# Keeping the residual of a four-layer decoder trunk transposed, and writing the mixer outputs transposed

## The chip, the cores and the metric

The kernel runs on one core of one Trainium2 chip. The metric is the device time of one launch in microseconds (us), lower is better. Three runs of the kernel before took 1474.31, 1475.74 and 1479.85 us; their median, 1475.74 us, is the time to compare with. The engines are named as the profile names them: PE (matrix products; PEld is its weight load), DVE (vector), ACT (scalar), POOL, and SP, which only starts transfers here.

## The reference

256 tokens of 1024 numbers pass through two layers of a mixer and an expert stage; every part adds its result to a residual `h`.

```python
h = x
for layer in range(2):
    xn = rmsnorm(h, norm_mix[layer])
    if layer == 0:
        h = h + attn_retention_mixer(xn, even_w_in, even_w_out)   # q, k, v, gate: 1024 -> 3584; out 1024 -> 1024
    else:
        h = h + short_conv_mixer(xn, odd_w_in, odd_conv, odd_w_out)  # 1024 -> 3072, gates, 3-tap conv, 1024 -> 1024
    h = h + peer(rmsnorm(h, norm_ffn[layer]), w_q, sub_keys, u, v)
return rmsnorm(h, final_norm)
```

`rmsnorm(x, g)` is `x / sqrt(mean(x*x) + eps) * g`. `peer` makes 8 query heads per token, takes the top 16 of 256 candidate experts of each head out of 16384 experts, and sums `gate * gelu(t . u[e]) * v[e]` over them.

## The kernel before, in words

**Precision.** Most products of full precision are three products: each factor is split into a high part (a cast on ACT, L176 for weights) and a low part in bf16 (a subtraction on DVE or POOL, L178). For an activation the high part and the remainder lie side by side in `x2` (8 blocks of 128 model dimensions, two parts, 256 tokens), a bf16 copy of the high part in `Xb`, cast by POOL.

**Weights.** `Stream` holds a list of all weight tiles in their order of use and a ring of 8 raw tiles of 512 KB. `st.next()` hands out the next tile and first calls `st.ahead`, which loads and splits tiles up to two beyond it; `st.parts()` splits one more; `st.next(ahead=False)` and `st.loads()` only take or load. The order of the instructions on every engine is the order of the program text: each engine takes its own in turn, and waits on semaphores for the others.

**Four stages, then four more.** (1) The even mixer: 28 weight tiles, attention and retention worked in between, then the output projection. (2) The expert stage `peer` of layer 0. (3) The odd mixer: 24 input tiles, convolution, output projection. (4) `peer` of layer 1, and the last norm.

**Output projection of a mixer** (`v_phase`, `v_mm`, L324 to L358). The result has the tokens on the partitions: four accumulators of 128 tokens by 512 dimensions, one PSUM bank each. The activation is the stationary operand, 128 columns of it, and the weight tile moves, 512 columns a product. Each of the eight weight tiles gives 12 products. The last two tiles are worked accumulator by accumulator, so that the four quarters of the result come out one after another.

**The norm behind a mixer** (`Norm`). Each quarter is added to `h` by DVE (L356), squared on ACT with a row sum (L397), and turned by PE, four transposes a call of `turn` (L445), because the next stage needs the model dimensions on the partitions. `parts` then makes `x2` (ACT L454, DVE L455) from the turned blocks. The transposes stand between the products of the last two weight tiles and inside the first pair of query tiles. `u_pair` (L308) multiplies two weight tiles with `x2` block by block and calls `tail(k)` behind each block k. The scale of the norm is applied later, to the scores.

**The expert stage.** For each of 16 query tiles f: a query product (`u_tile`), a copy to `qT` (L1312), and, one f later, the product with the keys (L1160), whose result is scaled on its way out of PSUM (L1163). `pump` deals the routing (top 16 of the scores, then of the pairs, the search for indices, the gates) to DVE in small pieces. For 160 of the 256 tokens the experts are worked densely: all 128 tiles of `u` (`dense_u`, L1417), the gelu, then all 128 tiles of `v` (L1520, L1560, L1562) into eight accumulators `vo`, one PSUM bank for each 128 model dimensions. For the other 96 tokens, rows of `u` and `v` are fetched by address (POOL L1029) and summed on DVE (L1039, L1050); `leave` (L1537) turns these sums into `vo`. `rows` (L522) makes what both paths read: `whole` and `scaled` (L528, L532) the dense activation out of `x2`, `fetched` (L535) the normalised rows out of `h`, `doubled` copies of them.

**The residual at the end of `peer`.** In steps 16 to 23 of the dense `v` phase PE adds the residual to `vo`, by a product of a block of `h` with the identity (L1550, L1551). The last three `v` tiles are worked block by block; `fold` (L1572) brings a block out of PSUM with an ACT copy (L1573) and a DVE sum of 160 columns (L1574) into `XT`, which is transposed. Behind layer 0, `Folded` makes `x2` out of `XT` (L576, L577) and has PE turn `XT` back in four groups of four transposes (`back`, L548), for the squares (L593) and for `h` (L609). Behind layer 1, `Final` squares the blocks, multiplies them with the gain, turns them and scales them.

**The start.** `x` comes with the tokens on the partitions in two transfers, one from SP and one from ACT; the small constants come before it, three weight tiles after it, all from SP. PE turns `x` (16 transposes), and `first` makes `x2` from the turned blocks with three weight splits in between; `late` sums the squares of `h` in steps 0 and 1.

The lines that a sentence does not say, the body of the projection before:

```python
for a in range(4):
    for j in range(2):
        run(v_mm(ws[j], ps[j], accs[a], a // 2, a % 2, False, j == 1))
        if a == 3 and j == 0:
            norm.amid()
    v.tensor_tensor(h[:, a // 2, ...], accs[a], h[:, a // 2, ...], OP.add)
    norm.done(a, accs[a])
```

## Time and profile before

| what | value |
|---|---|
| median of three runs | 1475.74 us (1474.31 to 1479.85) |
| the profiled execution, its own time | 1473.25 us |
| its span, first to last instruction | 1471.5 us |
| PE, PEld busy | 97%, 90% of the span |
| DVE, ACT, POOL busy | 84%, 55%, 53% |
| granted PE clock | 0.996 |
| read from memory | 527.93 MB, 359 GB/s over the span |
| even mixer, first product to last | 9.8 to 128.6 us |
| expert stage of layer 0 | 128.6 to 746.7 us |
| odd mixer | 746.7 to 844.2 us |
| expert stage of layer 1 and last norm | 844.2 to 1471.5 us |

How to read it: times in the rows are microseconds from the start of the span. A row of the timeline gives start, duration, engine, line, operation, output and inputs with their shapes, and the count that is merged into the row; behind it in brackets stands how long the engine had been idle, and what released it. PE's products are pipelined: one lasts some 0.3 to 0.6 us from end to end, but the next one starts much earlier. So the rate of PE is read from the distance between starts, not from the durations. Outside the span lie 1.75 us of the profiled execution (1473.25 less 1471.5).

### The profile page before, as it was taken

What the parts mean: (1) busy time and instruction counts of PE and PEld (TensorE: products, weight loads), DVE (VectorE), ACT (ScalarE), POOL (GpSimd) and SP (SyncE); (2) the same over time, 40 slices, a digit from 0 to 9 for tenths busy, and PEclk for the clock granted to TensorE, in tenths of its full rate; (3) what the DMA queues carried; (4) which work ended last, traced back from release to release, by engine and by line L of the source; (5) the groups of instructions that cost most, each with busy time, mean ns of one, the idle gap of its engine ahead of it and who ended that gap; (6) DMA issues with size and microseconds to landing.
All of it is one profiled execution on the core that took longest, in us unless ns stands there. A gap on an engine that the chain in (4) does not pass through costs nothing.

```text
span 1471.5 us, 29881 instructions
## 1 busy us (share of the span) xinstructions
PE 1426.3 (97%) x11246; PEld 1327.1 (90%) x11260; DVE 1238.5 (84%) x2505; ACT 804.0 (55%) x1872; POOL 779.3 (53%) x508
## 2 busy tenths in 40 slices
PE   9999999999999999999999999999999999999997
PEld 5667999999999999988998699999999999998887
DVE  5637999968898689989976589998788869999997
ACT  5555512248786556665563463212887746665654
POOL 6754545555655247655444374465555626665440
PEclk9999999999999999999999999999999999999999
DMA  8546899999999999999975588999999999999994
GB/s 325 191 156 247 315 370 392 400 414 411 409 406 404 400 393 412 415 416 414 411 264 181 180 303 342 403 382 406 409 412 413 410 411 392 408 415 414 415 415 181
DMA packets 113729, 531.78 MB, mean 361 GB/s; under 512 B 13168, under 2 KB 13424, under 8 KB 83888
## 3 DMA queue, kind: packets, MB, share of 16 engines
q1 hardware_dynamic: 57024, 325.06, 55.8%
q0 software_dynamic: 56416, 204.29, 35.1%
q8 instruction: 88, 1.44, 0.4%
q10 hardware_dynamic: 144, 0.52, 0.1%
q14 instruction: 57, 0.47, 0.1%
HBM read 527.93 MB, written 1.05 MB: 359 GB/s over the span
## 4 chain that ended last, share of the span: by engine, by line
PE 37%; DVE 23%; DMA 23%; issue 9%; POOL 6%; ACT 1%; DVEq 0%; SPq 0%; POOLq 0%; ACTq 0%
PE hid L1417 11%; DMA grow<-pvn,ig 9%; DMA rows<-pvn,ig 9%; PE vo L1560 5%; DMA rows<-pun,ig 4%; POOL rows L1029 4%; DVE rows L1039 4%; PE vo L1562 3%; PE hid L299 2%; PE vo L1520 2%; DVE hg L1149 2%; DVE hg L1155 2%; DVE hg L1151 2%; POOL grow L1029 2%; PE ea L331 2%
## 5 line engine op out<-in xcount | busy, mean ns | idle before, releaser
L1417 PE MATMUL hid<-xf,raw 128*128 128x160 f32 x3328 | 477.2, 301 | 7.8 <-DVE hg L1460 7.8
L1417 PEld LDWEIGHTS hid<-xf,raw 128*128 128x128 f32 x3328 | 457.8, 190 | 10.0 <-DVE hg L1460 9.9
L1428 ACT CAST vhi<-raw 128x1024 fp32r<-128x1024 f32 x222 | 229.9, 1047 | 191.7 <-DMA raw<-pv 96.7
L1029 POOL DMA_INDIRECT rows<-pvn,ig x128 | 217.7, 1700 | 183.9 <-DVE gacc L1050 150.1
L1435 DVE TENSOR_TENSOR vlo<-raw,vhi 128x1024 bf16<-128x1024 f32 x222 | 266.5, 1216 | 22.5 <-ACT vhi L1428 22.1
L1029 POOL DMA_INDIRECT rows<-pun,ig x128 | 163.4, 1277 | 116.1 <-DVE rows L1039 59.1
L1560 PE MATMUL vo<-ko,vhi 128*128 128x320 f32 x1200 | 213.6, 320 | 0.0
L178 POOL TENSOR_TENSOR lo<-raw,hi 128x1024 bf16<-128x1024 f32 x70 | 168.0, 2410 | 85.1 <-ACT hi L176 77.2
L1560 PEld LDWEIGHTS vo<-ko,vhi 128*128 128x128 f32 x1200 | 178.0, 189 | 0.0
L1562 PE MATMUL vo<-hb,vlo 128*128 128x160 bf16 x1776 | 162.0, 234 | 15.8 <-DVE vlo L1435 15.6
L1050 DVE SCALAR_TENSOR_TENSOR gacc<-rows,ghid,gacc 128x1024 f32<-128x1024 f32 x124 | 158.3, 1277 | 17.9 <-DMA rows<-pvn,ig 17.6
L1039 DVE SCALAR_TENSOR_TENSOR rows<-rows,xg 128x1024 f32<-128x1024 f32 x128 | 154.9, 1217 | 21.2 <-DMA rows<-pun,ig 20.9
L1029 POOL DMA_INDIRECT grow<-pvn,ig x64 | 117.7, 1838 | 94.7 <-DVE gacc L1050 77.2
L1457 ACT ACTIVATE hg<-hid 128x160 f32<-128x160 f32 (+14 forms) x240 | 61.9, 265 | 192.3 <-PE hid L1417 192.2
L1562 PEld LDWEIGHTS <-vlo 128*128 128x128 bf16 x1776 | 117.9, 98 | 42.4 <-DVE vlo L1435 22.2
L1029 POOL DMA_INDIRECT grow<-pun,ig x64 | 84.2, 1316 | 79.0 <-DVE grow L1039 51.9
L1367 ACT ACTIVATE ko<-ko,idxT 128x128 f16<-128x128 f16 x320 | 101.6, 391 | 38.3 <-DVE ko L1352 38.2
L176 ACT CAST hi<-raw 128x1024 fp32r<-128x1024 f32 x100 | 102.3, 1046 | 29.0 <-issue 17.4
L299 PE MATMUL hid<-x,hi 128*128 128x256 f32 x800 | 107.4, 287 | 3.9 <-DVE z L982 2.0
L299 PEld LDWEIGHTS hid<-x,hi 128*128 128x128 f32 x800 | 98.6, 190 | 5.0 <-issue 3.1
L1560 PE MATMUL vo<-xf,vhi 128*128 128x320 f32 x576 | 102.7, 321 | 0.0
L1370 ACT ACTIVATE ko<-ko,idxT 128x128 f16<-128x128 f16 x320 | 101.2, 389 | 0.0
(258 smaller groups left out, 2238.4 us busy)
## 6 DMA issues: line engine op xcount, KB each, us to landing
raw<-pv SPq DMA_DIRECT2D x128, 1024.0 KB, 9.4
raw<-pu SPq DMA_DIRECT2D x104, 1024.0 KB, 8.2
raw<-wq SPq DMA_DIRECT2D x32, 512.0 KB, 4.0
raw<-ew_in SPq DMA_DIRECT2D x28, 512.0 KB, 4.6
raw<-ow_in SPq DMA_DIRECT2D x24, 512.0 KB, 4.9
hg<-pe_ SPq DMA_DIRECT2D x22, 512.0 KB, 6.4
raw<-ew_out SPq DMA_DIRECT2D x8, 512.0 KB, 4.0
raw<-ow_out SPq DMA_DIRECT2D x8, 512.0 KB, 3.5
```

The lines of the kernel that those rows point to most:

```text
L176: self.nc.scalar.copy(hi, t)
L178: eng.tensor_tensor(lo, t, hi.bitcast(F32), OP.subtract)
L299: pe.matmul(ps[:, :S], hi[:, k * P:(k + 1) * P], A2[:, k, s_, :], start=k == 0 and s_ == 0, stop=False)
L1029: gp.indirect_dma_start(self.row(s_), None, table, bass.IndirectOffsetOnAxis(IG[:, 0, s_ % STEPS:s_ % STEPS + 1].bitcast(U32), 0))
L1039: v.scalar_tensor_tensor(r, r, 1.0, XG[:, q % 2, :], op0=OP.mult, op1=OP.mult, accum_out=w)
L1050: v.scalar_tensor_tensor(self.acc[q], r, w, self.acc[q], op0=OP.mult, op1=OP.add)
L1367: act.activation(hi[:, j], lo[:, j], AF.Copy, scale=idxT[:, 1, t:t + 1])
L1417: pe.matmul(ps[:, :TD], w[k], xv["xf"][:, k, :], start=k == 0, stop=k == ND - 1)
L1428: act.copy(whi[j], raw)
L1435: v.tensor_tensor(wlo[j], raw, whi[j].bitcast(F32), OP.subtract)
L1560: pe.matmul(vo[b][:, TG:S + TD], hi[:, b * P:(b + 1) * P], hs, **m)
L1562: pe.matmul(vo[b][:, TG:S], lo[:, b * P:(b + 1) * P], hb, **m)
```

## The change

`h` is now transposed from the first load to the last norm: 128 model dimensions on the partitions, eight blocks of 256 tokens. The host gives `x` in that form, and a second copy `xn` with the tokens on the partitions, which only the first norm's sums read.

- **Start.** The two halves of `x` and then the two of `xn` are loaded by ACT, the small table by POOL, three weight tiles and the constants by SP. PE turns nothing; `first` makes `x2` from `h` straight away. 28 idle products instead of 24 keep PE running before. `late` runs in steps 1 and 2.
- **Output projection.** The weight tile is stationary, the activation moves: per weight tile 16 products of the high part (two for each of eight blocks) and then eight of the low part, each with 256 columns. Block b lies in accumulator b % 4, half b // 4. The split of the first two query tiles is asked for one tile earlier (`st.ahead(2)`). The last two weight tiles are worked block by block.
- **Norms behind a part.** `Norm` serves all four: behind each block one or two DVE sums into `h`, ACT's high part, ACT's square (not summed), DVE's low part. Two DVE sums in `tail(2)` add the squares up over the blocks, and four products with a column of ones (`sums`, L540 of the changed kernel) add them up over the partitions, behind `u_pair` and ahead of whatever PE does next. There are no transposes between.
- **Expert stage.** `fetched_rows` turns the 96 fetched tokens back (eight transposes) and scales them. `dense` makes the dense activation in eight DVE operations of 160 columns, in place of one sum and one product of 1280. The products with the identity are gone; `fold` is two DVE operations.
- **Last norm.** The gain is applied by ACT, not DVE.

```diff
-    h = pers.tile([P, 2, D], F32, tag="h", name="h")
+    h = pers.tile([P, ND, S], F32, tag="h", name="h")
...
         accs = [acc_tile(i, nm("acc")) for i in range(4)]
+        def out_of(b):
+            return accs[b % 4][:, b // 4 * S:(b // 4 + 1) * S]
+        def high(b, w, p, first):
+            c = slice(b * P, (b + 1) * P)
+            m = dict(stop=False, skip_group_check=True)
+            pe.matmul(out_of(b), w[0][:, c], p[0], start=first, **m)
+            pe.matmul(out_of(b), w[0][:, c], p[1], start=False, **m)
+        def low(b, w, p, last):
+            pe.matmul(out_of(b), w[1][:, b * P:(b + 1) * P], p[2], start=False, stop=last, skip_group_check=True)
         for i in range(n - 2):
             each(i)
             w = st.next()
+            if i == n - 3:
+                st.ahead(2)
             p = part(i)
-            for a in range(4):
-                run(v_mm(w, p, accs[a], a // 2, a % 2, i == 0, False))
+            for b in range(ND):
+                high(b, w, p, i == 0 and b < 4)
+            for b in range(ND):
+                low(b, w, p, False)
...
-        ws = [st.next(), st.next(ahead=False)]
-        st.ahead(0)
+        ws = [st.next(ahead=False) for _ in range(2)]
+        st.loads()
...
+        norm.begin(lambda b: v.tensor_tensor(h[:, b, :], out_of(b), h[:, b, :], OP.add))
+        for b in range(ND):
+            for w, p in zip(ws, ps):
+                high(b, w, p, False)
+            for j, (w, p) in enumerate(zip(ws, ps)):
+                low(b, w, p, j == 1)
+            norm.block(b, [])
...
+    def fetched_rows(norm):
+        fq = [acc_tile(ch, nm("fq")) for ch in range(2)]
+        for b in range(ND):
+            pe.transpose(fq[b // 4][:TG, b % 4 * P:(b % 4 + 1) * P], h[:, b, :TG], ident)
+        for ch in range(2):
+            c = slice(ch * 512, (ch + 1) * 512)
+            v.scalar_tensor_tensor(XG[:TG, 0, c], fq[ch][:TG, :], norm.scale(0)[:TG], XG[:TG, 1, c],
+                                   op0=OP.mult, op1=OP.mult)
...
+        def block(self, b, pend):
+            self.fold(b)
+            self.high(b)
+            act.activation(self.sq[b // 4][:, b % 4 * S:(b % 4 + 1) * S], h[:, b, :], AF.Square)
+            if b:
+                self.low(b - 1)
+            if b == 5 and self.mixes:
+                st.parts()
+            if b == ND - 1:
+                self.low(b)
+        def tail(self, k):
+            if k == 1:
+                if self.mixes:
+                    st.parts()
+                else:
+                    st.ahead(0)
+            if k == 2:
+                a, b = self.sq
+                v.tensor_tensor(a, a, b, OP.add)
+                v.tensor_tensor(a[:, :2 * S], a[:, :2 * S], a[:, 2 * S:], OP.add)
+            if k == 7 and self.mixes:
+                st.parts()
+                st.parts()
...
+            def dense():
                 XF = new_xf()
                 ps = self.spread()
+                for k in range(ND):
+                    v.scalar_tensor_tensor(XF[:, k, :], h[:, k, TG:], self.gain(k), ps[:, TG:], op0=OP.mult, op1=OP.mult)
...
                 if f == 0:
                     pair = u_pair(xv["x2"], Xb, before.tail)
+                    before.sums()
...
-                m = dict(start=False, stop=False, skip_group_check=True)
-                if 16 <= i < 16 + ND:
-                    b = i - 16
-                    c = slice(b * P, (b + 1) * P)
-                    pe.matmul(vo[b][:, :P], h[:, 0, c], ident, **m)
-                    pe.matmul(vo[b][:, P:S], h[:, 1, c], ident, **m)
...
             def fold(b):
-                act.copy(XT[:, b, :], vo[b][:, :S])
-                v.tensor_tensor(XT[:, b, TG:], vo[b][:, S:S + TD], XT[:, b, TG:], OP.add)
+                v.tensor_tensor(h[:, b, :], vo[b][:, :S], h[:, b, :], OP.add)
+                v.tensor_tensor(h[:, b, TG:], vo[b][:, S:S + TD], h[:, b, TG:], OP.add)
...
-        nc.sync.dma_start(G, small)
-        nc.sync.dma_start(C[:, :P], cst[:, :P])
-        for th in range(2):
-            (nc.scalar if th else nc.sync).dma_start(h[:, th, :], x[th])
-        nc.sync.dma_start(C[:, P:], cst[:, P:])
+        gp.dma_start(G, small)
+        for a in range(2):
+            nc.scalar.dma_start(h[:, a * 4:(a + 1) * 4, :], x[:, a * 4:(a + 1) * 4, :])
...
+        for th in range(2):
+            nc.scalar.dma_start(XG[:, th, :], xn[th])
+        nc.sync.dma_start(C, cst)
-        busy(24)
+        busy(28)
```

Two places show how the order moves. The first is PE at the end of the even mixer, on the last two weight tiles. Before: `acc` is a quarter of the result, `c2e` and `cbe` the activation, `hi` and `lo` the parts of the weights, `xt` the turned residual.

```order
L333 MATMUL acc_990<-lo_1076,cbe 128x512
L445 MATMUL xt_1170<-cst,h 128x128
L445 MATMUL xt_1171<-cst,h 128x128
L445 MATMUL xt_1170<-cst,h 128x128
L445 MATMUL xt_1171<-cst,h 128x128
L331 MATMUL acc_991<-hi_1046,c2e 128x512
```

The same place now, from the low products of the third block to the high ones of the fourth:

```order
L351 LDWEIGHTS lo_1056
L351 MATMUL acc_975<-cbe,lo_1056 128x256
L351 LDWEIGHTS lo_1097
L351 MATMUL acc_975<-cbe,lo_1097 128x256
L347 MATMUL acc_976<-c2e,hi_1055 128x256
L348 MATMUL acc_976<-c2e,hi_1055 128x256
L347 MATMUL acc_976<-c2e,hi_1096 128x256
```

The transposes are gone, the operands have changed places, and a block takes six products of 256 columns. The second place is DVE where the even mixer passes into the expert stage. Before: `x` is `x2`, `nw` the sums and the scale of the norm, `lo` the low part of a query weight, `hg` the scores.

```order
L455 SCALAR_TENSOR_TENSOR x_1182<-xt_1171,small,x_1182 128x256
L414 SCALAR_TENSOR_TENSOR nw_176<-nw_176 128x1
L415 RECIPROCAL nw_176<-nw_176 128x1
L416 SCALAR_TENSOR_TENSOR nw_176<-nw_176 128x1
L417 TENSOR_SCALAR nw_176<-nw_176 128x1
L418 TENSOR_TENSOR nw_176<-nw_176 128x1
L178 TENSOR_TENSOR lo_1258<-raw,hi_1257 128x1024
L1147 MAX hg_1210<-hg_1210 128x8
```

And now (`xg` and `xf` hold the squares, `ssq` the sums over the partitions):

```order
L471 SCALAR_TENSOR_TENSOR x_1195<-h,small,x_1195 128x256 x2
L178 TENSOR_TENSOR lo_1314<-raw,hi_1313 128x1024
L527 TENSOR_TENSOR xg<-xg,xf_1196 128x1024
L528 TENSOR_TENSOR xg<-xg 128x512
L543 TENSOR_SCALAR nw_161<-ssq_1365 128x2
L545 RECIPROCAL nw_161<-nw_161 128x2
L546 TENSOR_TENSOR nw_161<-nw_161 128x2
L547 TENSOR_TENSOR nw_161<-nw_161 128x2
L548 TENSOR_SCALAR nw_161<-nw_161 128x2
L549 TENSOR_TENSOR nw_161<-nw_161 128x2
L1108 MAX hg_1287<-hg_1287 128x8
```

The split of the query weight now stands ahead of the norm's sums instead of behind them. On PE the four products that wait for these sums stand right behind the pair's last product, ahead of the first product with the keys:

```order
L321 MATMUL hid_1304<-xb,lo_1167 128x256
L540 MATMUL ssq_1365<-cst,xg 128x1 x4
L1121 MATMUL sc_1379<-ko_570,hg_1287 128x128 x2
L299 MATMUL hid_1400<-x_1195,hi_1313 128x256 x16
```

What was moved here is a wait: PE now reaches the first product with the keys only through the sums of the norm.

201 lines of the change are left out of this document (58 added, 143 removed).

## The prediction

> **What bounds the kernel now.** I read the page first, then busy times by stretch, then the timeline of each engine at the places that the change touches, then the waits.
>
> ```profile
> PE 1426.3 (97%) x11246; PEld 1327.1 (90%) x11260; DVE 1238.5 (84%) x2505; ACT 804.0 (55%) x1872; POOL 779.3 (53%) x508
> ```
>
> PE is busy nearly all the time, so PE work that goes is worth its time unless something else is late next. The dense `v` phases of the two layers, each in two stretches (columns: stretch, length, busy time of PE, PEld, DVE, ACT and POOL, granted clock, DMA share, GB/s):
>
> ```profile
> 500.00:620.00 120.00, 119.77 (x1056) 113.78 (x1055) 114.22 (x109) 75.82 (x94) 74.04 (x35) 1.00 1.01 403
> 620.00:738.00 118.00, 111.68 (x957) 104.59 (x955) 109.06 (x103) 69.39 (x86) 57.27 (x29) 0.99 1.01 413
> 1215.00:1330.00 115.00, 114.58 (x1004) 108.59 (x1001) 110.54 (x105) 71.11 (x88) 74.74 (x35) 1.00 1.01 405
> 1330.00:1452.00 122.00, 112.99 (x977) 105.59 (x978) 114.22 (x108) 71.12 (x89) 50.92 (x30) 1.00 0.99 402
> ```
>
> In the first half of each phase PE never stops (119.77 of 120 us). In the second it idles 6.3 and 9.0 us. Memory has next to nothing left: 403 to 413 GB/s at a DMA share of 1. So two resources bind there, first PE, then the transfers. The mixers and the passages between stages are bound by PE alone, or by what PE waits for.
>
> **Part 1, the products of the projection: nothing.** Old pattern, the starts of two successive weight tiles of the odd projection, and under them two query-like tiles (`u_tile`) of the odd mixer, which already have the new pattern (16 products of the high part, 8 of the low one, 256 columns):
>
> ```profile
> 822.67 0.58 PE L331 MATMUL acc<-hi,c2o 128*128 128x512 f32 x1
> ...
> 825.45 0.58 PE L331 MATMUL acc<-hi,c2o 128*128 128x512 f32 x1
> ```
>
> ```profile
> 760.05 2.15 PE L299 MATMUL hid<-x,hi 128*128 128x256 f32 x16
> ...
> 762.84 2.15 PE L299 MATMUL hid<-x,hi 128*128 128x256 f32 x16
> ```
>
> 12 products of 512 columns take 825.45 - 822.67 = 2.78 us, 24 of 256 take 2.79 us. I take 0 for the 16 tiles, and 2.79 / 8 * 2 = 0.70 us for a block of the last two tiles.
>
> [...]
>
> **Part 2, the end of the mixers.** From the first product of the last two weight tiles to the first product with the keys, even mixer, then odd:
>
> ```profile
> 121.10 0.58 PE L331 MATMUL acc<-hi,c2e 128*128 128x512 f32 x1
> ...
> 128.58 1.50 PE L316 MATMUL hid<-x,hi 128*128 128x256 f32 x8
> ```
>
> ```profile
> 135.70 0.71 PE L1160 MATMUL sc<-ko,hg 128*128 128x128 f32 x4 [0.22 <-ACT hg L1312]
> ```
>
> ```profile
> 837.24 0.58 PE L331 MATMUL acc<-hi,c2o 128*128 128x512 f32 x1
> ```
>
> ```profile
> 851.35 0.71 PE L1160 MATMUL sc<-ko,hg 128*128 128x128 f32 x4 [0.22 <-ACT hg L1312]
> ```
>
> That is 14.60 and 14.11 us. PE alone would now need 8 * 0.70 for the blocks (before: 7.48 us, with the transposes), about 4.0 for the pair's high products, 1.7 for the low ones: 11.3 us. But the sums of the norm now stand in PE's way, so DVE and ACT are followed:
>
> ```profile
> 121.28 2.57 DVE L178 TENSOR_TENSOR lo<-raw,hi 128x1024 bf16<-128x1024 f32 x1 [1.47 <-ACT hi L176]
> ```
>
> ```profile
> 743.68 0.47 DVE L577 SCALAR_TENSOR_TENSOR x<-xg,small,x 128x256 fp32r<-128x256 f32 x1
> ...
> 762.37 0.43 DVE L982 TENSOR_TENSOR z<-hid,y 128x256 f32<-128x256 f32 x1
> ```
>
> ```profile
> 743.10 0.51 ACT L576 ACTIVATE x<-xg,small 128x256 fp32r<-128x256 f32 x1
> ```
>
> ```profile
> 1454.89 0.42 ACT L641 ACTIVATE fin<-xg 128x256 f32<-128x256 f32 x1 [0.39 <-DVE xg L1574]
> ```
>
> ```profile
> L1236 DVE TENSOR_TENSOR hg<-hg 128x1024 f32<-128x1024 f32 x8 | 9.8, 1222 | 0.1
> ```
>
> A block costs DVE a sum (as L982, 0.43) and a low part (as L577, 0.47); neighbours overlap a little, I take 0.80 us, more than PE's 0.70. ACT (0.51 + 0.42) keeps up. In the odd mixer DVE starts 0.9 us behind the first block's start and ends with the eighth low part at 0.9 + 6.4 + 0.6 = 7.9. Then ACT splits the next query tile (about 1.05), DVE takes its low part (1.22), then the two sums of squares (1.22 and about 0.65): 12.1 us. PE has come to its four products at 11.3 and waits 0.8. These (0.5), the mean, the root on ACT and the copy of the first query (another 0.8) lead to the first product with the keys at 13.4: 0.7 earlier than 14.11. In the even mixer the DVE split in the first row ends at 123.85, 2.75 us behind the start; the split of the query tiles was asked for earlier, but ACT reached it at this place before as well, so I move nothing. DVE then runs 1.85 us later than in the odd one, and the first product with the keys comes at about 15.0, 0.4 later than before.
>
> What follows: eight transposes for the fetched rows,
>
> ```profile
> 748.69 1.04 PE L548 MATMUL fq<-cst,xg 128*128 128x128 f32 x8
> 749.48 2.15 PE L316 MATMUL hid<-x,hi 128*128 128x256 f32 x16
> ```
>
> 0.8 us for eight, 0.85 with the hand-over, on PE's path; and on DVE:
>
> ```profile
> 136.85 0.29 DVE L1147 MAX8 hg<-hg 128x8 f32<-128x128 f32 x1 [1.16 <-ACT hg L1163]
> ```
>
> ```profile
> 148.30 3.22 DVE L528 TENSOR_TENSOR xf<-x 128x1280 f32<-128x1280 f32 x1
> ...
> 154.86 1.47 DVE L532 TENSOR_TENSOR xf<-xf,rb 128x1280 f32<-128x1280 f32 x1
> ```
>
> ```profile
> 852.50 0.30 DVE L1147 MAX8 hg<-hg 128x8 f32<-128x128 f32 x1 [1.16 <-ACT hg L1163]
> ```
>
> The routing's first MAX8 stood 15.75 and 15.26 us behind the starts; now the scale is ready a microsecond behind the root, then a score is scaled: 16.25 and 14.65, so +0.5 and -0.6. The dense activation cost 4.69 us; eight operations of 160 columns with a PSUM operand, at most 0.33 each, cost 2.6: -2.0. The two engines meet at the end of the routing, where PE stands still:
>
> ```profile
> 293.68 2.44 PE L1417 MATMUL hid<-xf,hg 128*128 128x160 f32 x16 [1.48 <-ACT hg L1457]
> ```
>
> ```profile
> PE hid L1417 <- ACT hg L1457: 2.1, 1, 2.1
> ```
>
> (the second row is the waits of layer 1's stretch: 2.1 us, once). DVE's chain, for which ACT waits there, ends at -1.5 (even) and -2.6 (odd) against before; PE's own work at 0.4 + 0.85 = +1.25 and -0.7 + 0.85 = +0.15. The later of the two counts, and PE had 1.5 and 2.1 us to spare: **-0.3** for the even mixer (1.25 - 1.5), **-1.9** for the odd (0.15 - 2.1). If DVE's gain did not come, they would be +0.5 and -0.6; if both gains came in full, -1.5 and -2.6.
>
> **Part 3, the products with the identity.** One of the eight steps:
>
> ```profile
> 524.30 0.43 PE L1550 MATMUL vo<-cst,h 128*128 128x128 f32 x2
> ...
> 524.71 1.42 PE L1560 MATMUL vo<-xf,vhi 128*128 128x320 f32 x8
> ```
>
> 0.41 us, eight times: 3.3 us in each layer, in the half where PE is the bound. Behind it memory is. 403 GB/s in place of 413 over 120 us is 1.2 MB, or 2.9 us of transfers, that an earlier PE could pull forward. The ends are 0 (the transfers set the end) and -3.3. I take the middle, **-1.6** in each layer.
>
> **Part 4, the end of the first expert stage.**
>
> ```profile
> 738.37 0.46 PE L1538 MATMUL vo<-cst,gacc 128*128 128x96 f32 x2 [0.58 <-DVE gacc L1050]
> ...
> 746.68 2.18 PE L316 MATMUL hid<-x,hi 128*128 128x256 f32 x16
> ...
> 757.26 2.15 PE L299 MATMUL hid<-x,hi 128*128 128x256 f32 x16
> ```
>
> Sixteen transposes back (twice 0.8) leave PE. But DVE now has two sums and a low part a block, 1.1 us against PE's 1.04 (8.31 / 8), and the weight split at block 5 waits for ACT behind that block's square, 1.5 us on which DVE stands. The pair's last low part comes near 752.4, PE ends the pair at 754.4 (754.0 before), does the four sums, the third tile (2.8) and the spread of the scale, and starts the next tile at 758.2: **+0.9**; between -1 (no wait) and +1.5.
>
> **Part 5, the start.**
>
> ```profile
> 9.78 1.20 PE L331 MATMUL ea<-hi,x 128*128 128x512 f32 x4 [0.88 <-ACT hi L176]
> ```
>
> ```profile
> 16.17 7.17 POOL L178 TENSOR_TENSOR lo<-raw,hi 128x1024 bf16<-128x1024 f32 x3 [1.29 <-ACT hi L176]
> ```
>
> ```profile
> 21.35 0.58 PE L331 MATMUL ea<-hi,x 128*128 128x512 f32 x1
> ```
>
> ```profile
> 0.00:14.55 14.55, 11.93 (x61) 8.19 (x62) 5.68 (x11) 6.89 (x13) 3.19 (x8) 1.00 0.84 323
> ```
>
> Without the turn the first product can start at about 8.9 instead of 9.78. But 1 MB of `xn` shares the transfers: if both queues get half, the fourth weight tile is through when 4.7 MB have moved, that is at 14.55 us (323 GB/s). [...] **The last norm:** a multiplication goes from DVE to ACT, a copy from ACT to DVE; PE with its 1.25 us a block leads there. 0.
>
> **The sum:** 0.2 - 0.3 - 1.6 + 0.9 - 1.9 - 1.6 = -4.3 us. The profiled execution took 1473.25 us and would take 1468.95; it lies 2.5 us under the median of the runs shown, 1475.74, so I give 1471.4.
>
> **The rivals.** *PE's work counts in full.* Then both identity terms are -3.3, the mixers -1.5 and -2.6, the start -1 and part 4 zero: -11.7, 1464.0 us. For it speaks the unbroken PE in the first halves; against it DMA at a share of 1.
>
> *The transfers set the end.* Then what PE and DVE gain between 190 us and the stage's end is lost, and only PE's delays ahead of the saturated stretches count: 0.2 + 1.25 + 0.9 + 0.15 = +2.5, 1478.2 us. PE's idle time in the second halves speaks for it.
>
> *Slower: the weight loads show.* Every high product of the 16 projection tiles now loads its own weights under 256 columns, not 512.
>
> ```profile
> L299 PEld LDWEIGHTS hid<-x,hi 128*128 128x128 f32 x800 | 98.6, 190 | 5.0 <-issue 3.1
> ```
>
> A load takes 190 ns, a product's turn 116. Were the difference exposed at 256 products: 256 * 74 = +18.9 us, 1490.3 us. It eats the gain from 17 ns a load on (4.3 / 256). Against it: the odd mixer's tiles do just this, in 2.79 us. [...]
>
> **How the numbers follow.** A measurement of this kernel can tell about 0.5%, 7.4 us, from no change. The forecast gets 0.57, PE in full 0.24, the transfers 0.13, the loads 0.06. Faster by over 7.4 us needs the second case (0.24) or the forecast's lower end, a tenth of it (0.06): 0.30. Slower is the last case, 0.06; the rest is 0.64. The range runs from the second case, 1464.0, to a little over the third, 1479, with the spread of the runs in it.
>
> **What would show it.** Right: the tiles of the new projection at 2.8 us; PE waiting 1 us or so at the four sums (L540) behind the pair; the wait at the end of the routing gone or halved; PE idling more in the second halves of the dense phases by what the first halves gained. Wrong: a projection tile over 2.9 us, a wait at L540 over 3 us, or a dense phase that ends 3 us earlier with its transfers.

## The result and the profile after

| what | before | after |
|---|---|---|
| median (runs) | 1477.05 us (6) | 1495.98 us (6) |
| lowest to highest | 1473.48 to 1481.48 | 1492.55 to 1501.87 |
| span of the profiled execution | 1471.5 us | 1494.8 us |
| granted PE clock | 0.996 | 0.987 |

The ratio is 1.0132, with a 95% interval of 1.0108 to 1.0156: slower by 1.3%, where the forecast was 4.3 us faster. PE did not become less busy, it has longer to do the same:

```profile
PE 1431.1 (96%) x11359; PEld 1343.0 (90%) x11368; DVE 1254.8 (84%) x2523; ACT 800.2 (54%) x1857; POOL 773.5 (52%) x509
```

Where the 23.3 us of the two spans came in is read by cutting both timelines of PE at the same instructions (lengths in us). The last scores are the last product with the keys (L1160 before, L1121 after), the last blocks begin with the first product that brings the fetched experts' sums into `vo` (L1538, L1498), and the spread of the scale is the product that spreads the norm's scale over the partitions (L519, L555):

| stretch, by PE's first instruction of it | before | after | difference |
|---|---|---|---|
| start to the even projection | 103.67 | 105.89 | +2.2 |
| even projection to its last two tiles | 17.43 | 18.83 | +1.4 |
| last two tiles to the last scores | 63.99 | 70.12 | +6.1 |
| expert stage to its last blocks | 553.28 | 552.11 | -1.2 |
| last blocks to the spread of the scale | 18.52 | 23.53 | +5.0 |
| odd mixer to its last two tiles | 80.35 | 81.51 | +1.2 |
| last two tiles to the last scores | 63.51 | 67.27 | +3.8 |
| expert stage to its last blocks | 552.04 | 553.54 | +1.5 |
| last blocks to the end | 18.71 | 22.00 | +3.3 |

The loss lies in the short passages between the stages, a few us in each, and not in the 1100 us of the expert stages. The waits of PE in the changed kernel (who, for whom; us in all, times, the longest) name three of the places:

```profile
PE ssq L540 <- DVE xg L528: 6.4, 2, 3.3
PE ea L331 <- ACT hi L176: 3.2, 1, 3.2
PE hid L316 <- DVE x L471: 2.7, 4, 1.6
```

They come to 12 us, and the kernel before has none of them over 1 us. The rest is seen behind the even mixer, in PE's timeline of the changed kernel:

```profile
124.72 0.37 PE L347 MATMUL acc<-c2e,hi 128*128 128x256 f32 x1
...
135.42 0.50 PE L316 MATMUL hid<-x,hi 128*128 128x256 f32 x2 [0.36 <-DVE x L471]
135.77 1.92 PE L321 MATMUL hid<-xb,lo 128*128 128x256 bf16 x16
140.94 1.58 PE L540 MATMUL ssq<-cst,xg 128*128 128x1 f32 x8 [3.25 <-DVE xg L528]
143.27 1.22 PE L1121 MATMUL sc<-ko,hg 128*128 128x128 f32 x4 [0.75 <-ACT hg L1274]
144.15 3.76 PE L299 MATMUL hid<-x,hi 128*128 128x256 f32 x16
```

Two things are to be seen. PE stands 3.25 us at the four sums (L540). And what follows is slow by itself: 16 products took 2.15 us in the same stage before, here 3.76. The busy times by stretch (the third number from the right is the granted clock) say why:

```profile
136.00:141.00 5.00, 1.75 (x17) 1.36 (x14) 4.76 (x3) 0.94 (x1) 3.23 (x1) 1.00 0.72 270
141.00:143.20 2.20, 1.52 (x8) 1.43 (x8) 0.34 (x3) 0.45 (x3) 0.00 (x0) 0.55 0.81 294
143.20:145.00 1.80, 1.73 (x8) 1.73 (x9) 0.72 (x5) 0.76 (x4) 0.00 (x0) 0.50 0.59 232
145.00:148.00 3.00, 3.00 (x16) 2.84 (x16) 2.76 (x14) 1.09 (x2) 1.83 (x1) 0.50 0.00 0
```

Behind its wait PE worked at half clock for some 7 us. What it waited for stands in DVE's timeline of the same place, and beside it POOL's:

```profile
132.69 0.84 DVE L471 SCALAR_TENSOR_TENSOR x<-h,small,x 128x256 fp32r<-128x256 f32 x1
...
133.80 0.47 DVE L471 SCALAR_TENSOR_TENSOR x<-h,small,x 128x256 fp32r<-128x256 f32 x1
...
135.69 1.22 DVE L178 TENSOR_TENSOR lo<-raw,hi 128x1024 bf16<-128x1024 f32 x1 [0.32 <-ACT hi L176]
136.83 1.22 DVE L527 TENSOR_TENSOR xg<-xg,xf 128x1024 f32<-128x1024 f32 x1
138.09 2.71 DVE L528 TENSOR_TENSOR xg<-xg 128x512 f32<-128x512 f32 x1
```

```profile
132.65 0.61 POOL L474 CAST xb<-x 128x512 bf16<-128x512 f32 x1 [1.22 <-ACT x L466]
...
137.02 3.23 POOL L178 TENSOR_TENSOR lo<-raw,hi 128x1024 bf16<-128x1024 f32 x1 [1.93 <-ACT hi L176]
```

The second sum (L528), with half the columns of the first, takes 2.71 us: it ends 0.55 us behind POOL's low part (140.80 and 140.25). Every other low part of the activation (L471) takes 0.84 in place of 0.47 in the same way, where POOL's cast runs. Behind the odd mixer the second sum takes 2.71 us as well (863.81 to 866.52, POOL's low part from 862.80 to 865.97).

The same three things stand behind the expert stage of layer 0, again in PE's timeline of the changed kernel:

```profile
759.69 0.74 PE L316 MATMUL hid<-x,hi 128*128 128x256 f32 x4 [1.60 <-DVE x L471]
...
762.22 3.41 PE L321 MATMUL hid<-xb,lo 128*128 128x256 bf16 x16
765.82 1.04 PE L540 MATMUL ssq<-cst,xg 128*128 128x1 f32 x8 [0.19 <-issue]
...
770.48 0.68 PE L555 MATMUL rb<-cst,nw 128*128 128x128 f32 x4 [0.71 <-DVE nw L549]
```

Waits of 1.60, 0.35 and 0.36 us, then the low products in 3.41 us in place of 1.92.

The last norm shows another kind of loss, in DVE's timeline of the changed kernel:

```profile
1481.36 0.42 DVE L604 TENSOR_TENSOR xg<-xg 128x256 f32<-128x256 f32 x1 [0.54 <-ACT xg L601]
1481.71 0.41 DVE L1527 TENSOR_TENSOR h<-vo,h 128x256 f32<-128x256 f32 x1
1482.16 0.32 DVE L1528 TENSOR_TENSOR h<-vo,h 128x160 f32<-128x160 f32 x1
1483.02 0.43 DVE L604 TENSOR_TENSOR xg<-xg 128x256 f32<-128x256 f32 x1 [0.54 <-ACT xg L601]
```

1.66 us a block: DVE folds a block, stands 0.54 us until ACT has squared it, and sums before it folds the next. PE needs 1.26 us a block there.

At the start, PE's timeline of the changed kernel:

```profile
1.07 4.98 PE L395 MATMUL busy<-xb 128*128 128x256 bf16 x28 [1.07 <-DVE xb L1556]
9.28 2.07 PE L331 MATMUL ea<-hi,x 128*128 128x512 f32 x4 [3.23 <-ACT hi L176]
...
29.39 0.66 PE L736 MATMUL rtr<-cst,rt 128*128 128x128 f32 x4 [0.57 <-DVE rt L725]
```

The idle products end 3.23 us ahead of the first real one, and the first transposes behind the rotation, which need the norm's scale, come at 29.39; before they came at 27.11.

### The profile page after: what moved, and what is told of

It reads as the page before. It is cut to its first block, busy times and chain, and to the rows that moved or that the text cites. A ratio compares the mean times of both kernels' runs of the same rounds, so it can differ in the third digit from the quotient of the medians.

```text
span 1494.8 us, 30116 instructions
## 1 busy us (share of the span) xinstructions
PE 1431.1 (96%) x11359; PEld 1343.0 (90%) x11368; DVE 1254.8 (84%) x2523; ACT 800.2 (54%) x1857; POOL 773.5 (52%) x509
## 3 DMA queue, kind: packets, MB, share of 16 engines
HBM read 528.98 MB, written 1.05 MB: 355 GB/s over the span
## 4 chain that ended last, share of the span: by engine, by line
PE 37%; DVE 29%; DMA 21%; issue 8%; POOL 3%; ACT 2%; DVEq 0%; ACTq 0%; POOLq 0%; SPq 0%
PE hid L1379 13%; DMA rows<-pvn,ig 8%; DMA grow<-pvn,ig 8%; PE vo L1514 5%; DVE rows L1000 4%; PE hid L299 3%; PE vo L1516 3%; DMA rows<-pun,ig 2%; DVE vlo L1397 2%; DVE gacc L1011 2%; DVE grow L1000 2%; DVE hg L1110 2%; DVE hg L1112 2%; PE vo L1480 2%; DVE hg L1116 2%
## 5 line engine op out<-in xcount | busy, mean ns | idle before, releaser
L990 POOL DMA_INDIRECT rows<-pvn,ig x128 | 210.2, 1642 | 192.8 <-DVE gacc L1011 155.8
L1516 PE MATMUL vo<-hb,vlo 128*128 128x160 bf16 x1776 | 162.0, 234 | 20.8 <-DVE vlo L1397 20.5
L990 POOL DMA_INDIRECT grow<-pvn,ig x64 | 121.5, 1899 | 93.3 <-DVE gacc L1011 77.0
L990 POOL DMA_INDIRECT grow<-pun,ig x64 | 79.9, 1249 | 80.2 <-DVE grow L1000 50.1
L299 PE MATMUL hid<-x,hi 128*128 128x256 f32 x800 | 111.1, 293 | 3.5 <-DVE z L943 2.0
L299 PEld LDWEIGHTS hid<-x,hi 128*128 128x128 f32 x800 | 102.2, 197 | 4.3 <-issue 2.4
```

Source lines behind the costliest of these rows:

```text
L299: pe.matmul(ps[:, :S], hi[:, k * P:(k + 1) * P], A2[:, k, s_, :], start=k == 0 and s_ == 0, stop=False)
L990: gp.indirect_dma_start(self.row(s_), None, table, bass.IndirectOffsetOnAxis(IG[:, 0, s_ % STEPS:s_ % STEPS + 1].bitcast(U32), 0))
L1516: pe.matmul(vo[b][:, TG:S], lo[:, b * P:(b + 1) * P], hb, **m)
```

## The experiments

My theory: order and cover cost the time. In each passage a low part on DVE or POOL stands ahead of what PE waits for; DVE stands while POOL works; and PE's wait halves its own clock. The rivals: the transfers take up such gains and losses, so that repairing a passage returns little; the clock falls with the chip's load; or the removed products were worth their full 6.6 us and only hidden. In the expectations TensorE, VectorE, ScalarE and GpSimd are PE, DVE, ACT and POOL of the rows. All ratios are to the kernel before; the changed kernel stands at 1.0132. Losses in a stretch are given against the kernel before.

### Products that fill PE's waits

```diff
+            if not self.mixes:
+                fill = side_tile(nm("fill"))
+                for _ in range(26):
+                    pe.matmul(fill[:, :S], Z[:, :P], Z, start=True, stop=True)
             ssq = side_tile(nm("ssq"))
...
-        busy(28)
+        busy(44)
```

> Changed kernel with idle products added on TensorE: 16 more in the row ahead of the first weight tile, and 26 of 256 columns ahead of the four sums behind each mixer, where TensorE stood 3.25 and 3.10 us. Nothing waits less by this. Theory (TensorE's clock is granted at half for some 4 us once it has stood for 2 to 3 us): the first tile's products come at full pace, and the score, tile and low products behind the sums too (the 16 products of the first tile behind them in 2.15 us, in place of 3.76 and 3.22); about 2 us at the start, 2.8 and 1.9 us behind the mixers: 6.5 us less than the changed kernel, a ratio to the kernel before near 1.009. Rival (the clock falls because of the load of the chip, not because TensorE stood): the same stretches stay at half clock, and the ratio stays at 1.013 or rises.

Ratio 1.0115 (1.0077 to 1.0153). PE's timeline at the start, and behind the two mixers:

```profile
9.30 1.20 PE L331 MATMUL ea<-hi,x 128*128 128x512 f32 x4 [0.54 <-ACT hi L176]
...
29.58 0.66 PE L740 MATMUL rtr<-cst,rt 128*128 128x128 f32 x4 [2.66 <-DVE rt L729]
...
145.00 2.16 PE L299 MATMUL hid<-x,hi 128*128 128x256 f32 x16
...
867.53 3.34 PE L299 MATMUL hid<-x,hi 128*128 128x256 f32 x16
```

In the first tile and behind the even mixer the clock stayed up (four products in 1.20 us in place of 2.07, and 1.00 from 143 to 147 us), as the theory has it; behind the odd mixer it fell (0.60 from 866 to 870 us), although PE had worked until 864.6. So this run alone doesn't settle the clock. And at the start nothing was won: PE came earlier, waited 2.66 us for the norm's scale at the transposes, and the clock fell behind that wait (a product of L331 took 0.99 us at 30.61, 0.58 ahead of the wait).

### The sums first on DVE

```diff
             if k == 1:
+                a, b = self.sq
+                v.tensor_tensor(a, a, b, OP.add)
+                v.tensor_tensor(a[:, :2 * S], a[:, :2 * S], a[:, 2 * S:], OP.add)
+            if k == 2:
                 if self.mixes:
                     st.parts()
+                    st.parts()
                 else:
                     st.ahead(0)
```

> Changed kernel with VectorE's two sums of squares put ahead of the weight splits behind all three passages (the split at block 5 of the expert stage moves behind them too). Theory (the passages lose because VectorE reaches the sums late: it does a low part first, and its second sum then stands 2 us behind GpSimd's split): the second sum takes 0.65 us in place of 2.71, TensorE waits less than 1 us at the four sums, no stretch behind them is at half clock, and some 5 us come back at each mixer, 4 at the expert stage: 14 us less than the changed kernel, ratio 1.003. Rival (the passages' delays are taken up by the transfers later, so that the order of the sums matters little): waits at the sums gone as well, but the time falls by under 4 us, ratio 1.010 or more. Second rival (the sum over halves of one tile is slow by itself): it still takes 2.7 us, and TensorE still waits 1 to 2 us.

Ratio 1.0114 (1.009 to 1.0139). PE's timeline behind the even mixer, then DVE's:

```profile
137.90 0.95 PE L539 MATMUL ssq<-cst,xg 128*128 128x1 f32 x8
141.52 1.22 PE L1120 MATMUL sc<-ko,hg 128*128 128x128 f32 x4 [2.66 <-ACT hg L1273]
142.39 3.76 PE L299 MATMUL hid<-x,hi 128*128 128x256 f32 x16
```

```profile
136.92 0.69 DVE L521 TENSOR_TENSOR xg<-xg 128x512 f32<-128x512 f32 x1
137.53 3.37 DVE L178 TENSOR_TENSOR lo<-raw,hi 128x1024 bf16<-128x1024 f32 x1
```

The second sum takes 0.69 us now, so it is not slow by itself. The low part behind it takes 3.37 in its place, POOL's runs beside it, and the chain of the scale stands behind that low part on DVE. The wait moved from the four sums to the first scores, and the half clock with it. The theory's size failed, its mechanism showed at the next instruction.

### POOL's part taken away, in two ways

The first try gave the fourth query tile's low part a later place in the program:

```diff
-                    st.ahead(0)
+                    st.parts()
+                    self.lows = []
+                    st._split(self.lows)
...
+            run(self.lows)
```

`_split` with a list puts the low part into it; the list is run at the end of `sums`, behind the scale's chain.

> Changed kernel with one instruction moved at each mixer's end: the low part of the fourth query tile on GpSimd is issued behind the chain of the norm's scale, in place of ahead of it; VectorE's order stays as it was, its low part still ahead of the two sums. Theory (VectorE's operation with two SBUF operands cannot run while GpSimd runs one, and the sum over halves stands until GpSimd's is done): that sum takes 0.69 us in place of 2.71, and TensorE waits 1.2 us at the four sums in place of 3.25 and 3.10. Rival (that sum is late because of the order on VectorE, and GpSimd only shares in it): 2.7 us and waits over 2.5 us stay. In all some 4 us under the changed kernel if the clock stays up, ratio near 1.010.

Ratio 1.0118 (1.01 to 1.0136), and the edit did not do what it says: POOL has nothing else in its queue there, so it started at 136.98 us as before (137.02), when ACT's high part was done; DVE's second sum took 2.71 us again and PE waited 3.25. A later place in a queue that stands empty is no later time. The second try leaves the whole split, ACT's part too, to the next tile:

```diff
-                    st.ahead(0)
+                    st.parts()
```

> Changed kernel with the split of the fourth query tile (high part on ScalarE, low part on GpSimd) not issued behind a mixer, but by the third tile, behind the scores of the first query. VectorE's order stays: the third tile's low part, then the two sums. Theory (an operation of VectorE on two SBUF operands stands while GpSimd works): the sum over halves takes 0.69 us in place of 2.71 and the wait at the four sums falls from 3.25 and 3.10 us to 1.2; the halves of the clock there go or shrink. Rival (the order on VectorE alone does it): the sum over halves still takes over 2 us, and the wait stays over 2.5 us. In all 4 to 6 us under the changed kernel if theory holds, ratio 1.009 to 1.0105.

Ratio 1.010 (1.0082 to 1.0118). DVE's timeline behind the even mixer, then PE's:

```profile
137.09 1.22 DVE L527 TENSOR_TENSOR xg<-xg,xf 128x1024 f32<-128x1024 f32 x1
138.34 0.69 DVE L528 TENSOR_TENSOR xg<-xg 128x512 f32<-128x512 f32 x1
```

```profile
139.18 1.02 PE L540 MATMUL ssq<-cst,xg 128*128 128x1 f32 x8 [1.24 <-DVE xg L528]
```

POOL's operation is gone from this place, and with it ACT's high part of the same split, which in the changed kernel had ended before the sum began (136.9 and 138.09 us). The sum falls from 2.71 to 0.69 us and the wait from 3.25 to 1.24 (1.08 behind the odd mixer): POOL's operation was the 2 us. The half clock goes behind the odd mixer (1.00 from 866 to 872 us) and lasts 3.4 us in place of 6.8 behind the even one. Both inputs of this sum lie in SBUF. A sum of the same 512 columns with one input in PSUM (L725 of the changed kernel, at 28.65 and 30.95 us) took 0.69 us although POOL's low parts ran beside it from 27.21 to 43.70 us.

### The passages in another order

A first form had the sums first, one low part behind them, and the other low parts behind the chain of the scale in the program; the splits at block 5 and in `tail` before were gone:

```diff
             if k == 1:
+                a, b = self.sq
+                v.tensor_tensor(a, a, b, OP.add)
+                v.tensor_tensor(a[:, :2 * S], a[:, :2 * S], a[:, 2 * S:], OP.add)
+                st._split()
+                self.lows = []
+                for _ in range(3 if self.mixes else 1):
+                    st._split(self.lows)
```

> Changed kernel with the two sums of squares first on VectorE, one weight split behind them, and the low parts of the other splits (one at a mixer's end, three at the expert stage's) behind the chain of the norm's scale; their high parts stay early on ScalarE. Theory (the passages lose because VectorE's low parts stand, GpSimd's among them, ahead of the sums or of the scale's chain, and TensorE's wait then halves its clock): no wait over 1 us between the pair of query tiles and the third tile, no stretch at half clock there; 4 to 5 us less at each of the three passages, 13 us under the changed kernel, ratio 1.004. Rival (the chain of the scale itself, some 2 us from the sums over mean and root to the copy of the query, is too long whatever stands ahead of it): waits of 2 us or more stay, some of the clock drops too, and only 4 to 6 us come back, ratio 1.009.

Ratio 1.0085 (1.0066 to 1.0104), near the rival's 1.009 and not the theory's 1.004. It left no profile to compare, so there are only times. By the first try above its edit had no hold on POOL; the same passages inside a larger collection (below) show POOL's low part beside DVE's as before. The second form leaves POOL's split to the next tile, too, and copies the first two queries ahead of the sums; in the odd mixer the low part of the fourth tile goes to DVE for that:

```diff
             if k == 1:
+                a, b = self.sq
+                v.tensor_tensor(a, a, b, OP.add)
+                v.tensor_tensor(a[:, :2 * S], a[:, :2 * S], a[:, 2 * S:], OP.add)
+                st.parts()
+                self.lows = []
+                if self.mixes:
+                    st._split(self.lows)
+                    st._split(self.lows)
...
-    srcs += [(ow_in[f], i > 1 and i % 2 == 1) for i, f in enumerate(OF)]
+    srcs += [(ow_in[f], i > 3 and i % 2 == 1) for i, f in enumerate(OF)]
...
                 if f == 0:
                     pair = u_pair(xv["x2"], Xb, before.tail)
+                    for q, ps in zip(qT, pair):
+                        act.copy(q, ps[:, :S])
                     before.sums()
```

> Changed kernel with the passages put in another order: the two sums of squares first on VectorE, then one low part; the split that GpSimd takes part in comes behind the scale's chain, since ScalarE makes its high part only then (at the expert stage the second tile's low part goes to VectorE for that); the copies of the first two queries stand ahead of the chain. Theory (these orders are what the passages lose): TensorE waits under 0.5 us between the pair and the tile behind it, no half clock; the first product with the keys comes some 4 us earlier than the changed kernel's at both mixers, the stretch from the pair to the spread of the scale takes 11 us in place of 15.3; 14 us in all, ratio 1.0035. Rival (a chain that cannot be reordered, mean, root and scale, still holds the routing, whose first MAX8 then moves by under 2 us, and the end of the routing by less): 1.008 or more.

Ratio 1.0054 (1.0039 to 1.0069). The expected returns came: from the even projection to the last scores 81.83 us (before 81.42, changed 88.95), from the last blocks to the spread 17.77 (18.52, 23.53), from the odd projection to the last scores 78.28 (80.05, 84.03), with no half clock at the three places. So neither the transfers nor the scale's chain held them. The edit took 4.6 us back in the odd mixer, though: 69.37 us from the spread to the projection, where the changed kernel takes 64.75. The waits of PE there make up nearly all of it: 2.46, 2.26 and 1.48 us, the first two with 3.4 us of half clock (1.7 us of work) behind each; in the changed kernel 1.98 and 1.48, the first with half clock.

### The start

```diff
-        busy(28)
+        busy(44)
...
-                    (5, rope_tr(0, 0)),
-                    (6, rope_tr(0, 1)),
+                    (6, rope_tr(0, 0)),
+                    (7, rope_tr(0, 1)),
```

> Changed kernel with 16 more idle products at the start and the first two transposes behind the rotation put one weight tile later. Theory (the start loses because the norm's scale is ready 2.4 us later, with its squares one tile later, and TensorE waits for it at these transposes; the half clock of the first tile only hides that): no wait at the transposes, and the first product of the projection comes within 1 us of the kernel before's 103.67 us; ratio 1.0115. Rival (the megabyte for the squares sets the start): TensorE waits for weight tiles instead, and that product stays at 105.9 us or later, ratio 1.013.

The first product of the projection came at 103.84 us (before 103.67, changed 105.89), with no wait at the transposes: the scale's later coming and the half clock of the first tile were the loss at the start. The two edits were not run apart, but the idle products without the later transposes had won nothing above. The ratio is 1.0105 (1.0083 to 1.0127).

### The last norm

```diff
-            sq = self.SQ[:, 1 if b else 0, :]
+            sq = self.SQ[:, 2 - b % 2 if b else 0, :]
...
-            if 0 < b < ND - 1:
-                v.tensor_tensor(self.SQ[:, 0, :], self.SQ[:, 0, :], sq, OP.add)
+            if b > 1:
+                v.tensor_tensor(self.SQ[:, 0, :], self.SQ[:, 0, :], self.SQ[:, 2 - (b - 1) % 2, :], OP.add)
```

> Changed kernel with the last norm's running sum on VectorE issued one block later (a third buffer for the squares), so that VectorE no longer waits in each block for ScalarE's square. Theory (the loop VectorE fold, ScalarE square, VectorE sum of 1.66 us a block sets the end of the last norm, where TensorE needs 1.26): the end comes 3.3 us earlier from the first block on, 18.7 us in place of 22.0; ratio 1.011. Rival (TensorE, or the last transfers, set that end): no change, ratio 1.013, with VectorE waiting elsewhere.

From the last blocks to the end 19.3 us (1470.40 to 1489.7), in place of 22.0. DVE's timeline:

```profile
1478.04 0.42 DVE L604 TENSOR_TENSOR xg<-xg 128x256 f32<-128x256 f32 x1
1478.60 0.42 DVE L1527 TENSOR_TENSOR h<-vo,h 128x256 f32<-128x256 f32 x1
1479.06 0.32 DVE L1528 TENSOR_TENSOR h<-vo,h 128x160 f32<-128x160 f32 x1
1479.30 0.41 DVE L604 TENSOR_TENSOR xg<-xg 128x256 f32<-128x256 f32 x1
```

1.26 us a block, PE's own pace. The ratio, 1.0129 (1.0108 to 1.015), cannot tell 2.7 us from none; the rows can.

### All of it, with and without the identity products

A first collection held the edits of the start and the last norm, the first form of the passages, and the first tile of each projection taking the blocks in the order 0, 1, 4, 5, 2, 3, 6, 7, so that it starts in the two banks that the gate's copies don't hold:

```diff
-            for b in range(ND):
+            for b in (0, 1, 4, 5, 2, 3, 6, 7):
                 high(b, w, p, i == 0 and b < 4)
```

> Changed kernel with the edits on the passages, on the start and on the last norm together, and with the projection's first tile taking the two banks first that the gate's copies do not hold. Theory (the change lost by four places in which order and cover were wrong, and what it removed is worth about 1 us a layer): the losses of 23 us come down to some 3 us, ratio 1.002 (0.999 to 1.005). Rival (the transfers pace the whole, and a gain in a passage is lost in the dense phases behind it): single gains do not add up, ratio 1.006 or more.

1.0043 (1.0028 to 1.0059): two thirds of the loss come back. PE still waited 2.66 and 2.60 us at the first scores, just as in the run with the sums first, which had no hold on POOL either. With the second form of the passages:

> The edits on the passages, on the start, on the banks of the first projection tile and on the last norm together. Theory (the losses were in order and cover only): what is left against the kernel before are eight transposes for the fetched rows at each mixer (0.85 us each) and 0.6 us at the last norm, against 1 to 2 us a layer of the removed identity products: ratio 0.999 to 1.001. Rival (the dense phases, paced by the transfers, keep what the passages give back): 1.003 or more, with TensorE idling more in the dense phases.

0.999 (0.9975 to 1.0004). To price what the change removed, the 16 identity products were put back into each dense phase, first in the changed kernel, then in this one:

```diff
+                if 16 <= i < 16 + ND:
+                    b = i - 16
+                    m = dict(start=False, stop=False, skip_group_check=True)
+                    pe.matmul(vo[b][:, :P], ident, h[:, b, :P], **m)
+                    pe.matmul(vo[b][:, P:S], ident, h[:, b, P:], **m)
```

> Changed kernel with the kernel before's 16 identity products put back into each dense phase, at the same place; they add the residual a second time, so the sums that follow are of other values. Theory (what the removed products freed was lost again to the transfers in the second half of the phase): under 1 us a layer more, ratio 1.013 to 1.014, and TensorE idles some 3 us less in the second half of each phase. Rival (TensorE's work counts in full, and the saving was there but hidden by the losses elsewhere): 3.3 us a layer more, 6.6 us, ratio 1.0175.

> The kernel with all those edits, and the 16 identity products put back into each dense phase; they add the residual a second time, so the values that follow are others. Theory (their removal is worth about half of their 3.3 us a layer, the rest goes to the transfers): 2 to 3 us over the kernel without them, 0.0015 to 0.002 in the ratio. Rival one (worth nothing): no more than 0.0005. Rival two (worth all): 6.6 us, 0.0045.

In the changed kernel 1.0133 (1.011 to 1.0157), which can't be told from 1.0132; each interval is some 3.5 us wide to either side, so this pair is too blunt to tell 3 us from none. In the repaired one 1.0015 (1.0003 to 1.0027) against 0.999: the medians lie 2.7 us apart (1476.82 and 1474.11), and from the first `v` product to the last blocks the two layers take 496.0 and 491.5 us. Over all the traces this stretch takes 494.5 to 496.0 us in the three kernels with the products (mean 495.2) and 490.6 to 494.9 in the twelve without (mean 492.6). So the removal is worth some 2.7 us for both layers by either way, near the middle between nothing and 6.6. The intervals of the pair touch, so a part of it stays uncertain. Where the rest goes is not shown: PE's waits for the low parts of `v` were 20.5 us in the changed kernel and 15.4 with the products put back, but 16.3 and 17.2 in the repaired pair.

Two points were left: the odd mixer, and the clock. For the first, one more split is asked for in the odd mixer, which the edit on the passage had taken away:

```diff
                     load_keys(1)
+                    st.parts()
```

> The kernel with all edits and one more weight split asked for early in the odd mixer, behind the first product with the scale. In the kernel without it the odd mixer took 67.9 us from the spread of the scale to the projection, the kernel before 63.8, with three splits of ScalarE in a row and VectorE's low parts behind GpSimd's. Theory (the edit on the passage took that split away from its place, and the mixer pays it on VectorE): 64 us again, 4 us less, ratio 0.996 to 0.997. Rival (the dense phase behind it keeps them): 0.998 or more.

0.998 (0.9966 to 0.9993): a little faster than the kernel before, but not to be told from the 0.999 without the split. The stretch in question takes 66.96 us in place of 68.04, not 64: a quarter of what the theory claimed. PE's waits name the 3 us that stay against the kernel before: 5.46 us in place of 3.87 in the stretch, and behind one of them, 2.26 us long, 3.4 us of half clock that cost 1.7. The kernels by stretch (lengths in us; passages = second form):

| stretch | before | after | passages | this one |
|---|---|---|---|---|
| start to the even projection | 103.67 | 105.89 | 105.81 | 103.96 |
| to the last scores | 81.42 | 88.95 | 81.83 | 81.37 |
| to the last blocks | 553.28 | 552.11 | 552.63 | 551.56 |
| to the spread of the scale | 18.52 | 23.53 | 17.77 | 18.08 |
| to the odd projection | 63.81 | 64.75 | 69.37 | 66.96 |
| to the last scores | 80.05 | 84.03 | 78.28 | 78.29 |
| to the last blocks | 552.04 | 553.54 | 554.93 | 550.34 |
| to the end | 18.71 | 22.00 | 21.58 | 19.34 |

For the clock, the same kernel was made to wait by a chosen length:

```diff
                 v.tensor_tensor(a, a, b, OP.add)
+                for _ in range({1: 1, 3: 3}.get(self.gi, 0)):
+                    v.tensor_tensor(b, b, b, OP.add)
```

> The same kernel with VectorE held between the two sums of squares by additions that nothing reads: one of 1.22 us at the even mixer, three at the odd one, so that TensorE waits some 1 us and some 3.4 us at the four sums, at places that are alike otherwise. Theory (TensorE's clock falls to half for some 4 us behind a wait of its own of over about 2 us): full clock at the even mixer, the next tile's 16 products in 2.15 us; half clock at the odd one, 3 us or more for them. Rival (the clock falls with the load of the chip at these places): both alike.

PE's timeline behind the even mixer and behind the odd one:

```profile
136.20 1.02 PE L538 MATMUL ssq<-cst,xg 128*128 128x1 f32 x8 [0.82 <-DVE xg L524]
...
137.53 2.16 PE L300 MATMUL hid<-x,hi 128*128 128x256 f32 x16
...
855.25 1.29 PE L538 MATMUL ssq<-cst,xg 128*128 128x1 f32 x8 [3.18 <-DVE xg L524]
...
857.25 3.06 PE L300 MATMUL hid<-x,hi 128*128 128x256 f32 x16
```

Behind a wait of 0.82 us the clock is 1.00, behind 3.18 us it is 0.58 (856 to 860 us), in a kernel that shows no half clock at either place without the added waits. So it is PE's own wait that brings it here, and not the load. This is one execution; how surely a wait of a given length does it is counted over all traces at the end.

## Why the prediction was wrong

- **The products of the projection, 0: right.** The starts of two successive tiles in the changed kernel:

```profile
109.86 0.36 PE L347 MATMUL acc<-c2e,hi 128*128 128x256 f32 x1
...
112.65 0.36 PE L347 MATMUL acc<-c2e,hi 128*128 128x256 f32 x1
```

  2.79 us, as forecast; the rival of the weight loads is refuted. That the loss came nevertheless is the failure: the forecast had thought of one way to lose over 0.5%, and it was not the way. What it didn't see is the even mixer's first tile, which took 3.97 us, with a wait of 0.57 us for a bank that ACT still read.
- **The end of the mixers, -0.3 and -1.9: wrong, and the largest error.** The step that failed is "about 0.65" for the second sum of squares. Up to there DVE's chain was near: from PE's first product of the first block to the end of the first sum it took 11.79 us in the odd mixer (11.4 by the forecast's terms) and 13.33 in the even one (13.25). The second sum then took 2.71 us in both, 2.06 more than forecast, beside POOL's low part. A block on DVE was mis-sized too (eight took 8.1 us, 1.01 each, in place of 0.80), but by the end of the first sum little of that was left.

  Behind the wait came what the forecast had no term for: half the clock, for 6.8 us behind the even mixer and 3.4 behind the odd one, which costs 3.4 and 1.7 us of work. PE's own path was to be +1.25 and +0.15 us there; with these two terms it would be +6.7 and +3.9, and to the last scores it was +6.1 and +3.8.

  PE was to wait 1 us or so at L540 and waited 3.25 and 3.10, over the 3 us that the forecast named as its refutation. (Two smaller misses: the four products that were given 0.5 us took 1.58 and 1.05, and the even mixer's 13.4 and 1.85 make 15.25, not 15.0.) The wait at the end of the routing did shrink as forecast, from 1.5 and 2.1 us to 0.9 and 0.2.

  That an operation on DVE can have two prices stood in the trace of before. Its group of the low parts reads

```profile
L577 DVE SCALAR_TENSOR_TENSOR x<-xg,small,x 128x256 fp32r<-128x256 f32 x8 | 5.2, 655 | 0.4 <-ACT x L576 0.2
```

  a mean of 0.655 us, where the prediction quoted one row of 0.47: the fast one of two kinds. The three slow ones of 0.92 are those that met POOL's cast (one starts at 742.61, the cast at 742.63).
- **The end of the first expert stage, +0.9: the right sign, much too small.** It took +5.0. The wait at the split of block 5 was seen (PE stood 1.60 us there), and its price was put at the wait alone; the clock (3.41 us for 1.92 us of products), the second sum (2.73) and a low part of 3.38 us on DVE ahead of the scale's chain had no term.
- **The identity products, -1.6 in each layer: about right.** The changed kernel's stretches show -1.2 and +1.5 with the dense phases in them, which is within what such stretches scatter (548.9 to 555.6 us in the twelve traces without the products); the pair of runs with and without them gives some 2.7 us together, for which 3.2 was said. That lies between the rivals of PE's work in full and of the transfers. The forecast had no other reason for the middle than that it is the middle, so the hit is in part luck.
- **The start, +0.2: wrong by 2 us.** No run shows this term, a price of the transfers: with the transfers as they are, more idle products and the first transposes one tile later bring the start back to 103.84 us. What the runs showed in its place is the norm's scale, whose last operation starts at 26.87 us in place of 24.48, and the 3.23 us gap behind too few idle products, with the clock at half behind it.
- **The last norm, 0: wrong by 3.3 us.** "PE with its 1.25 us a block leads there" added up each engine's work and overlooked the loop between two of them. Without the loop 2.7 us came back; the last 0.6 stay open.

The kernel with all edits runs at 0.998: by the ratio 1 to 5 us under the kernel before, about what the forecast had given the change itself. That the two are so near is in part luck, since its odd mixer still loses 3 us that the forecast did not have. But what failed was the cover and the order, not the worth of the removed work. The edits on the start and on the last norm alone were too small for a ratio; there the rows had to tell.

## What to carry to other kernels

Cost an operation on DVE by the mean and the spread of its group, not by one row, and look at what POOL does beside it: a DVE operation with two inputs in SBUF and a POOL operation stood in each other's way here (on DVE 2.71 us in place of 0.69 beside a low part, 0.84 in place of 0.47 beside a cast; on POOL 3.23 in place of 2.4), and the price fell on PE, which waited 3.25 us at the four sums. Where a change puts a wait on PE, follow it to the instructions behind it: here about every second wait of around 2 us, and nearly every one of 3 us, cost another 1.7 us or more in clock. Count a loop between two engines, A's result to B and B's back to A within one block, as a sum, not as the larger of the two.

## What the runs showed of the hardware that was not expected

- **When a wait halves the clock.** In the fifteen traces PE's clock falls to half 71 times before the last norm, each time for 3.4 us or for twice that (1.7 or 3.4 us of work), and each time during or just behind a wait of PE: a single one of 1.6 us or more, or in three cases several shorter ones close together (1.24 and 0.75 us with 1.0 us of one-column products between them, in the run that leaves the split to the next tile). But not every wait does it:

| length of PE's wait | waits | with half clock behind |
|---|---|---|
| 1.3 to 1.6 us | 90 | 0 |
| 1.6 to 1.9 us | 31 | 7 |
| 1.9 to 2.2 us | 36 | 23 |
| 2.2 to 2.5 us | 27 | 15 |
| 2.5 to 2.9 us | 12 | 8 |
| 3.0 us or more | 16 | 15 |

  Between 1.6 and 2.9 us the length alone doesn't decide. The same wait at the same place of the odd mixer, in PE's timeline of the kernel before and then of the changed one:

```profile
796.45 2.14 PE L299 MATMUL hid<-x,hi 128*128 128x256 f32 x16 [1.98 <-DVE z L982]
```

```profile
809.62 3.25 PE L299 MATMUL hid<-x,hi 128*128 128x256 f32 x16 [1.98 <-DVE z L943]
```

  Of the nine kernels with this wait of 1.98 us six show half clock behind it and three don't. In the changed kernel that is the +1.2 us of the odd mixer in the first table.
- **The kernel before has such drops too.** The clock is 0.66 from 460 to 465 us and from 685 to 690 us there, behind waits of 2.30 and 2.01 us. Up to the last norm PE stood at half clock for 6.8 us in the kernel before and for 30.7 in the changed one. The difference is 12 us of work, half of the 23.3 us of the spans if PE was the bound all that time.
- **POOL is slowed too.** POOL's low part of 1024 columns took 3.23 us beside DVE's sums behind the even mixer of the changed kernel, 2.36 to 2.40 nearly everywhere else there. Operations of one column suffer as well: in the norm's chain at the start two of them took 2.23 and 2.12 us (21.17 and 23.62 us of the changed kernel) beside POOL's low parts, 0.22 and 0.16 without. The kernel before has the same (2.05 and 2.12 us, at 18.96 and 21.24), so they are not this loss.
